# Moving the attention's product with the sigmoid from VectorE to GpSimd, with one operand of the scan in PSUM and other PSUM banks

## Chip, cores and metric

The kernel runs on one core of one Trainium2 chip (trn2). The metric is the device time of one execution, in microseconds (us). TensorE's matrix products are called PE here, its weight loads PEld, VectorE is DVE in the rows, ScalarE ACT, GpSimd POOL, and SP is the queue that issues the DMAs.

## What is computed

One decoder layer on x of shape 2048 x 1024, in float32. A projection gives the inputs of three kinds of mixer; their outputs are normalised by head group, multiplied by an output matrix, added to x and layer-normalised; then follow a feed-forward with squared relu and a second layer norm. The part that the change touches is the attention with 8 heads of 64 columns:

```python
z = jnp.einsum('bhtd,bhsd->bhts', qb, kb) * scale
mask = s_pos < t_pos
log_om = jnp.where(mask, jax.nn.log_sigmoid(-z), 0.0)
tail = lax.cumsum(log_om, axis=3, reverse=True) - log_om
log_a = jax.nn.log_sigmoid(z) + tail
a = jnp.where(mask, jnp.exp(log_a), 0.0)
outs.append(jnp.einsum('bhts,bhsd->bhtd', a, vb))
```

So the weight of position s for position t is sigmoid(z[t, s]) times the product of sigmoid(-z) over all positions between s and t.

## The kernel before

All large products are made with float32 operands split into a high and a low half, three products for each (high with high, high with low, low with high). ScalarE makes the high half by a copy, VectorE or GpSimd the low half by a subtraction. The positions are cut into four chunks of 512.

The program has two phases. Phase 1 holds the projections (`proj_t`, lines 224 to 226, and `proj_v`, lines 239 to 241), the attention, the short convolution and the pooling mixer (`bchp`), and the output product with the first layer norm (`out_stage`, product in lines 509 to 511, norm in lines 105 and 106). Phase 2 is the feed-forward (lines 656 to 679), which the change does not touch.

The attention works in score tiles, called units here: 128 positions t (index j) against up to 512 positions s of one chunk (index sg), for one head. There are 320 of them. For a head and a chunk c the tiles run from sg = c (the diagonal segment, where the four tiles are 128 to 512 wide) down to sg = 0 (each 512 wide). `unit` does this for one tile:

- PE makes z in one bank of PSUM (line 422, two products).
- ScalarE writes beta = sigmoid(-z) (line 425, one of two tiles in turn) and sig = sigmoid(z) (line 427, two tiles).
- VectorE runs a scan over beta from the right, which gives the running product in g. In the diagonal segment (line 432) the second operand is a constant tile `last`; in the other segments (line 434) the start value is one column of the g before, and the second operand is ignored, so beta is given twice.
- VectorE multiplies g by sig (line 436).

`block` then takes 128 positions s of a segment: PE transposes the four g's into one bank tp (line 453), ScalarE copies that to th (line 456), VectorE makes the low half tl (line 457), and PE adds v times th and v times tl to o (lines 458 and 459). `run` emits the blocks some five units after their tiles. `finish` takes o out (lines 472 and 473) and starts the head group's norm, whose statistics and transposes use the banks of tp too, and whose inverse root runs on VectorE in nine steps on 128 x 8 values (lines 73 to 75).

The attention uses six banks of PSUM: two for z, three for tp, one for o; the dense products have two (dn). The attention is emitted at a higher priority than the dense work of the mixers, and a scheduler, which times the program by its own model, writes each engine's order; each engine then works through its order without changing it. GpSimd has in phase 1 mostly low halves of x and of the weights (line 173: `low_engine` gives two of three to GpSimd at first and one of three to VectorE), and the sums of the pooling mixer. The transposes before the feed-forward (`transposed`, line 579) take banks of tp as well.

Of the kernel before, what the change touches and what calls it, by code (L numbers as in the profile page):

```python
# [9 lines left out]
F = mybir.dt.float32  # L10
# [3 lines left out]
ALU = mybir.AluOpType  # L14
# [3 lines left out]
P = 128  # L18
# [3 lines left out]
CH = 512  # L22
# [10 lines left out]
OFF = 8  # L33
# [8 lines left out]
def build(nc, tc, ctx, A, out):  # L42
    const = ctx.enter_context(tc.tile_pool(name="const", bufs=1))
    dram = ctx.enter_context(tc.tile_pool(name="dram", bufs=1, space=DRAM))

    nc.scalar.preload_act_table_set("sigmoid_and_others")
    ident = const.tile([P, P], F, name="ident")
    make_identity(nc, ident)
    eps_ln = const.tile([P, 1], F, name="eps_ln")
    nc.vector.memset(eps_ln, LN_EPS)  # L50

    qscr = [[dram.tile([2, HD, CH], F, name=f"qscr{c}_{h}") for h in range(HEADS)] for c in range(NC)]
    kscr = [[dram.tile([2, HD, CH], F, name=f"kscr{c}_{h}") for h in range(HEADS)] for c in range(NC)]
    vscr = [[dram.tile([4, P, 4, P], F, name=f"vscr{c}_{g}") for g in range(2)] for c in range(NC)]
    mscr = [[dram.tile([P, CH], F, name=f"mscr{c}_{j}") for j in range(ND)] for c in range(NC)]
    x1scr = [[dram.tile([P, D], F, name=f"x1scr{c}_{t}") for t in range(4)] for c in range(NC)]
    tscr = [[dram.tile([P, 4, ND, P], F, name=f"tscr{c}_{i}") for i in range(2)] for c in range(NC)]

    def split(dst_hi, dst_lo, src, scale=None):
        if scale is None:  # L60
            nc.scalar.copy(dst_hi, src)
            nc.vector.tensor_tensor(dst_lo, src, dst_hi.bitcast(F), ALU.subtract)
        else:
            nc.scalar.activation(dst_hi, src, AF.Identity, scale=scale)
            nc.vector.scalar_tensor_tensor(dst_lo, src, scale, dst_hi.bitcast(F), ALU.mult, ALU.subtract)

    def rsqrt(pool, var, eps, shape, tag):
        """1 / sqrt(var + eps): a first value from the bits of the operand, then three Newton steps."""
        v, s, t = (pool.tile(shape, F, name=f"{tag}{k}", tag=f"{tag}{k}", bufs=2) for k in "vst")
        nc.vector.tensor_scalar(v, var, eps, None, ALU.add)  # L70
        nc.vector.tensor_scalar(s.bitcast(I), v.bitcast(I), 1, 0x7FFFFFFF, ALU.logical_shift_right, ALU.bitwise_xor)
        for _ in range(3):
            nc.vector.scalar_tensor_tensor(t, s, SEED * SEED, s, ALU.mult, ALU.mult)
            nc.vector.scalar_tensor_tensor(t, t, -0.5, v, ALU.mult, ALU.mult)
            nc.vector.scalar_tensor_tensor(s, t, 1.5, s, ALU.add, ALU.mult)
        return s

    def ln_stats(p, t, inverse):
        st = p.tile([P, 2, 6], F, name="st", tag="st", bufs=2)
        for i in range(2):  # L80
            nc.vector.bn_stats(st[:, i, :], t[:, i * 512:(i + 1) * 512])
        mv = p.tile([P, 2], F, name="mv", tag="mv", bufs=2)
        nc.vector.bn_aggr(mv, st)
        return mv[:, 0:1], inverse(p, mv[:, 1:2])

    def inverse_dve(p, var):
        s = rsqrt(p, var, LN_EPS, [P, 1], "ln")
        nc.vector.tensor_scalar(s, s, SEED, None, ALU.mult)
        return s

    def inverse_act(p, var):
        y, t = (p.tile([P, 1], F, name=f"ln{k}", tag=f"ln{k}", bufs=2) for k in "yt")
        nc.scalar.activation(y, var, AF.Ln, bias=eps_ln)
        nc.scalar.activation(y, y, AF.Exp, scale=-0.5)
        nc.scalar.activation(t, y, AF.Square)
        nc.vector.scalar_tensor_tensor(t, var, LN_EPS, t, ALU.add, ALU.mult)  # L96
        nc.vector.tensor_scalar(t, t, -0.5, 1.5, ALU.mult, ALU.add)  # L97
        nc.vector.tensor_tensor(y, y, t, ALU.mult)  # L98
        return y

    def layer_norm(p, t, g, b):
        m, y0 = ln_stats(p, t, inverse_dve)
        for i in range(2):
            h = t[:, i * 512:(i + 1) * 512]
            nc.vector.scalar_tensor_tensor(h, h, m, g[i], ALU.subtract, ALU.mult)
            nc.vector.scalar_tensor_tensor(h, h, y0, b[i], ALU.mult, ALU.add)

    def bcast(p, name):
        t = p.tile([P, D], F, name=name)
        nc.sync.dma_start(t, A[name].partition_broadcast(P))  # L110
        return t

    with ExitStack() as c1:
        ff, first = phase1(nc, tc, c1, A, ident, (qscr, kscr, vscr, mscr, x1scr, tscr), split, rsqrt, layer_norm, bcast)
        phase2(nc, tc, c1, A, ff, first, x1scr, lambda p, t: ln_stats(p, t, inverse_act), bcast, out)


def phase1(nc, tc, ctx, A, ident, scr, split, rsqrt, layer_norm, bcast):
# [3 lines left out]
    pp = att.enter_context(tc.tile_pool(name="attps", bufs=1, space=PSUM, reuse_waits="tile"))  # L122
# [23 lines left out]
    for i in range(2):  # L146
        w = pd.tile([P, P], F, name=f"pw{i}")
# [26 lines left out]
        return h, l  # L174

    def load_w(g, x=None):
        """The halves of group g of w_in, with the tiles of chunk x between them as the products take them."""
        w, xt = [], []
        with early():
            for q in range(4):  # L180
                w.append(load(A["w_in"][g][q], "w", [P, 2, 256], ND))
                if x is not None:
                    xt += [load_x(x, d) for d in (2 * q, 2 * q + 1)]
        return w, xt
# [5 lines left out]
    later = []  # L190
# [11 lines left out]
        return ppd.tile([P, CH], F, name="dn", tag="dn", bufs=2)  # L202

    def operands(xs, g):
        """Yields the halves of group g of w_in with those of x for each chunk, loaded at the first use."""
        w = None
        for c, x in xs:
            if w is None:
                w, xt = load_w(g, None if x else c)
                x += xt  # L210
            elif not x:
                with early():
                    x += [load_x(c, d) for d in range(ND)]
            yield c, w, x
# [149 lines left out]
    pend, soon = [], []  # L364

    betas = []
    for i in range(2):
        t = p.tile([P, CH + 1], F, name=f"beta{i}")
# [8 lines left out]
                head(c, 2 * i + hh, mix)  # L377

    def run(end=False):
        """Emits the queued score tiles, each block of weights a few of them later."""  # L380
        while units:
            units.pop(0)()
            turn[0] += 1
            if turn[0] > 5:
                blocks.pop(0)()
        while end and blocks:
            blocks.pop(0)()
            turn[0] = 0
        while end and soon:
            soon.pop(0)[1]()  # L390
# [17 lines left out]
    def unit(c, h, sg, m, j, st, start):  # L408
# [8 lines left out]
            m.update(k=k.bitcast(R), v=v.bitcast(R), g=[])  # L417
        q = st["q"].bitcast(R)
        w = (j + 1) * P if diag else CH
        z = pp.tile([P, CH], F, name="z", tag="z", bufs=2)  # L420
        for b in range(2):
            nc.tensor.matmul(z[:, 0:w], q[:, b, j * P:(j + 1) * P], m["k"][:, 0:w], start=(b == 0), stop=(b == 1))  # L422
        beta = betas.pop(0)
# [2 lines left out]
        sig = p.tile([P, CH], F, name="sig", tag="sig", bufs=2)  # L426
# [4 lines left out]
        if diag:  # L431
            nc.vector.tensor_tensor_scan(left, rev, last[:, :CH + OFF - w - 2:-1], 0.0, ALU.mult, ALU.add)
        else:
            nc.vector.tensor_tensor_scan(left, rev, rev, st["prev"][j][:, OFF - 1:OFF], ALU.mult, ALU.bypass)  # L434
        gv = g[:, OFF:OFF + w]
        nc.vector.tensor_tensor(gv, gv, sig[:, 0:w], ALU.mult)  # L436
        st["prev"][j] = g
        m["g"].append(g)

    def block(c, h, sg, m, b, st, mix):  # L440
# [6 lines left out]
            st["o"] = pp.tile([P, CH], F, name="o", tag="o", bufs=1)  # L447
        o, v = st["o"], m["v"]
        t0 = b * P if diag else 0
        tp = pp.tile([P, CH], F, name="tp", tag="tp", bufs=3)  # L450
        cols = slice(OFF + b * P, OFF + (b + 1) * P)
        for j in range(b if diag else 0, 4):
            nc.tensor.transpose(out=tp[:, j * P:(j + 1) * P], in_=m["g"][j][:, cols], identity=ident)
# [12 lines left out]
    def finish(c, h, o, mix):  # L466
        if h % 2 == 0:
            mix["t"] = p.tile([P, CH], F, name="mixr", tag="mixr", bufs=2)
        t = mix["t"]
        own = slice((h % 2) * HD, (h % 2) * HD + HD)  # L470
        other = slice(HD - own.start, P - own.start)
        nc.scalar.copy(t[own], o[other])
        nc.vector.tensor_tensor(t[own], o[own], t[own], ALU.add)
        if h % 2:
            pend.append(rms(t, h // 2, c, lambda: pp.tile([P, CH], F, name="msp", tag="tp", bufs=3), "a"))

    wo = []

# [86 lines left out]
    def ff_pool():  # L565
        return ctx.enter_context(tc.tile_pool(name="x1", bufs=1, reuse_waits="tile"))

    spare = [(pp, 3)]

    def spare_ps():  # L570
        pool, bufs = spare[-1]
# [50 lines left out]
class FeedForward:  # L622
# [20 lines left out]
        return [[t[:, d] for d in range(ND)] for t in w]  # L643

    def hidden(self, f, w=None):
        """Squared relu of the up projection for hidden tile f, in halves."""
        nc, p = self.nc, self.p
        wh, wl = w or self.up(f)
        hh = p.tile([P, HALF], R, name="hh", tag="hh", bufs=4)
# [15 lines left out]
        return hh, hl  # L665

    def rows(self, f):
        """The rows of w_down for hidden tile f, in halves."""
        return self.split(self.pd.tile([P, D], R, name="dh", tag="dh", bufs=4),
                          self.pd.tile([P, D], R, name="dl", tag="dl", bufs=4),  # L670
                          self.raw(self.A["w_down"][f * P:(f + 1) * P, :]))
# [97 lines left out]
```

## Time and profile before

| what | value |
|---|---|
| runs, median (lowest to highest) | 2616.57 us (2616.32 to 2616.8), 3 runs |
| profiled execution: span from its first to its last instruction | 2613.2 us |
| outside the span, against the median | 3.4 us |
| mean granted clock of TensorE | 0.987 |
| first dense product, 20th unit, last unit, first product of the down projection | 4.5, 92.8, 1005.5, 1227.8 us |

The page gives for the profiled execution its span; a time of its own beside that is not listed, so the 3.4 us are the distance to the median. In the rows, a group is a line of the program, an engine, an operation, and the tiles written and read; "x" is how often. Busy time of PE is made of records that overlap, since products are pipelined.

### The profile page before, as it was taken

How to read it: one execution, taken by the hardware profiler on the slowest of the kernel's cores; microseconds unless marked ns; L12 is line 12 of the kernel's file. 1: busy time of each engine (PE TensorE's matmuls, PEld its weight loads, DVE VectorE, ACT ScalarE, POOL GpSimd, SP SyncE). 2: the span in 40 equal slices, each digit the busy share in tenths (PEclk: the TensorE clock that was granted, in tenths of full speed). 3: DMA queues.
4: the chain of work that ended last, by engine and by line, in shares of the span. 5: the costliest groups of instructions: out<-in, count | busy, mean ns of one | idle time of the engine just before them, and what ended most of it. 6: DMA issues, size and time to landing. Idle time of an engine off the chain costs nothing. (4 is left out here: it accounts for less than half of the span.)

```text
span 2613.2 us, 32747 instructions
## 1 busy us (share of the span) xinstructions
PE 2519.7 (96%) x12112; PEld 2080.0 (80%) x12112; DVE 1718.6 (66%) x2839; ACT 982.4 (38%) x1802; POOL 558.9 (21%) x293
## 2 busy tenths in 40 slices
PE   8999999889989988999999999999999999999998
PEld 7887888768767767878888888888888888888886
DVE  4899999999999998875444444443564444444437
ACT  4667666656566563212221212121332121212122
POOL 2012000330131030211221212121342121212122
PEclk9999999999999999999999999999999999999999
DMA  8658545523342342668211111110541111111111
GB/s 243 176 153 227 151 134 142 180 74 101 101 121 78 93 133 90 229 215 322 91 57 41 57 41 57 41 57 25 217 154 57 41 57 41 57 41 57 41 41 65
DMA packets 131584, 280.63 MB, mean 107 GB/s; under 512 B 14944, under 2 KB 31328, under 8 KB 130400
## 3 DMA queue, kind: packets, MB, share of 16 engines
q1 hardware_dynamic: 131424, 278.54, 33.8%
q8 instruction: 95, 1.56, 0.2%
q14 instruction: 65, 0.53, 0.1%
HBM read 211.64 MB, written 66.85 MB: 107 GB/s over the span
## 5 line engine op out<-in xcount | busy, mean ns | idle before, releaser
L704 DVE TENSOR_TENSOR y<-dn,y 128x512 f32<-128x512 f32 x448 | 303.9, 686 | 367.0 <-PE dn L679 366.6
L677 PE MATMUL dn<-dh,hh 128*128 128x512 f32 x1024 | 398.3, 389 | 0.6 <-ACT hh L662 0.6
L678 PE MATMUL dn<-dl,hh 128*128 128x512 f32 x1024 | 398.4, 389 | 0.0
L679 PE MATMUL dn<-dh,hl 128*128 128x512 f32 x1024 | 398.2, 389 | 0.0
L656 PE MATMUL up<-x,uh 128*128 128x512 f32 x1008 | 392.3, 389 | 0.0
L657 PE MATMUL up<-x,uh 128*128 128x512 f32 x1008 | 392.2, 389 | 0.0
L663 DVE SCALAR_TENSOR_TENSOR rl<-up,rl 128x512 f32<-128x512 f32 x128 | 88.5, 691 | 374.6 <-ACT hh L662 374.6
L632 POOL TENSOR_TENSOR ul<-raw,uh 128x1024 fp32r<-128x1024 f32 x63 | 152.0, 2414 | 770.1 <-PE up L659 608.5
L661 ACT ACTIVATE rl<-up 128x512 f32<-128x512 f32 x128 | 76.2, 596 | 498.0 <-PE up L659 498.0
L434 DVE TENSOR_TENSOR_SCAN g<-beta,g 128x513 f32<-128x513 f32 x192 | 257.1, 1344 | 1.4 <-ACT beta L425 1.2
L659 PE MATMUL up<-x,ul 128*128 128x512 f32 x1008 | 256.2, 389 | 0.0
L173 POOL TENSOR_TENSOR wl<-wraw,wh 128x512 fp32r<-128x512 f32 x67 | 104.6, 1567 | 622.4 <-ACT wh L171 372.1
L436 DVE TENSOR_TENSOR g<-g,sig 128x512 f32<-128x512 f32 (+2 forms) x320 | 223.1, 702 | 11.4
L677 PEld LDWEIGHTS dn<-dh,hh 128*128 128x128 f32 x1024 | 192.2, 188 | 41.2 <-ACT hh L662 1.0
L679 PEld LDWEIGHTS dn<-dh,hl 128*128 128x128 f32 x1024 | 192.1, 188 | 40.3 <-DVE hl L664 0.4
L678 PEld LDWEIGHTS dn<-dl,hh 128*128 128x128 f32 x1024 | 192.2, 188 | 39.9
L224 PE MATMUL dn<-xh,wh 128*128 128x512 f32 x512 | 211.9, 416 | 11.4 <-ACT xh L171 4.8
L659 PEld LDWEIGHTS up<-x,ul 128*128 128x128 f32 x1008 | 189.2, 188 | 39.3
L657 PEld LDWEIGHTS up<-x,uh 128*128 128x128 f32 x1008 | 189.2, 188 | 39.3
L656 PEld LDWEIGHTS up<-x,uh 128*128 128x128 f32 x1008 | 189.2, 188 | 39.2
L225 PE MATMUL dn<-xl,wh 128*128 128x512 f32 x512 | 209.9, 410 | 0.1
L425 ACT ACTIVATE beta<-z 128x512 f32<-128x512 f32 (+2 forms) x320 | 173.4, 542 | 96.7 <-PE z L422 56.0
(159 smaller groups left out, 4603.8 us busy)
## 6 DMA issues: line engine op xcount, KB each, us to landing
raw<-in_w_down SPq DMA_DIRECT2D x64, 512.0 KB, 3.3
raw<-in_w_up SPq DMA_DIRECT2D x63, 512.0 KB, 3.3
wraw<-in_w_in SPq DMA_DIRECT2D x80, 256.0 KB, 3.0
k<-kscr SPq DMA_DIRECT2D x80, 256.0 KB, 3.1
v<-vscr SPq DMA_DIRECT2D x80, 256.0 KB, 2.8
xraw<-in_xt SPq DMA_DIRECT2D x64, 256.0 KB, 3.0
q<-qscr SPq DMA_DIRECT2D x64, 256.0 KB, 4.3
x<-tscr SPq DMA_DIRECT2D x8, 2048.0 KB, 12.3
```

What stands on the lines that cost most here:

```text
L224: nc.tensor.matmul(ps, wh, xh, start=(d == 0), stop=False)
L225: nc.tensor.matmul(ps, wh, xl, start=False, stop=False)
L425: nc.scalar.activation(beta[:, CH - w:CH], z[:, 0:w], AF.Sigmoid, scale=-1.0)
L434: nc.vector.tensor_tensor_scan(left, rev, rev, st["prev"][j][:, OFF - 1:OFF], ALU.mult, ALU.bypass)
L436: nc.vector.tensor_tensor(gv, gv, sig[:, 0:w], ALU.mult)
L656: nc.tensor.matmul(ps, wh[d], xh[:, :, d, :], start=(d == 0), stop=False)
L657: nc.tensor.matmul(ps, wh[d], xl[:, :, d, :], start=False, stop=False)
L659: nc.tensor.matmul(ps, wl[d], xh[:, :, d, :], start=False, stop=(d == ND - 1))
L677: self.nc.tensor.matmul(ps, hh[:, ts], dh[:, ds], start=(i == 0), stop=False)
L678: self.nc.tensor.matmul(ps, hh[:, ts], dl[:, ds], start=False, stop=False)
L679: self.nc.tensor.matmul(ps, hl[:, ts], dh[:, ds], start=False, stop=(i == len(hid) - 1))
L704: nc.vector.tensor_tensor(y[t][:, ds], ps, y[t][:, ds], ALU.add)
```

## The change

The product of g and sig is issued on GpSimd instead of VectorE. In the segments off the diagonal the ignored second operand of the scan is the first column of z in PSUM, repeated, instead of beta; so the scan reads one tensor from SBUF and one from PSUM, and z's bank is free only when the scan is done. The bank that z gains, tp loses: three for z, two for tp, also where the norms and the transposes before the feed-forward use them.

```diff
-        z = pp.tile([P, CH], F, name="z", tag="z", bufs=2)
+        z = pp.tile([P, CH], F, name="z", tag="z", bufs=3)
...
         else:
-            nc.vector.tensor_tensor_scan(left, rev, rev, st["prev"][j][:, OFF - 1:OFF], ALU.mult, ALU.bypass)
+            idle = z[:, 0:1].to_broadcast([P, CH + 1])
+            nc.vector.tensor_tensor_scan(left, rev, idle, st["prev"][j][:, OFF - 1:OFF], ALU.mult, ALU.bypass)
         gv = g[:, OFF:OFF + w]
-        nc.vector.tensor_tensor(gv, gv, sig[:, 0:w], ALU.mult)
+        nc.gpsimd.tensor_tensor(gv, gv, sig[:, 0:w], ALU.mult)
...
-        tp = pp.tile([P, CH], F, name="tp", tag="tp", bufs=3)
+        tp = pp.tile([P, CH], F, name="tp", tag="tp", bufs=2)
...
-            pend.append(rms(t, h // 2, c, lambda: pp.tile([P, CH], F, name="msp", tag="tp", bufs=3), "a"))
+            pend.append(rms(t, h // 2, c, lambda: pp.tile([P, CH], F, name="msp", tag="tp", bufs=2), "a"))
...
-    spare = [(pp, 3)]
+    spare = [(pp, 2)]
```

The new lines shift the numbers by one: the scan stands in line 435, the product in 437, the transposes in 454, th in 457, tl in 458, the products with v in 459 and 460, the output products in 510 to 512. The scheduler writes new orders for all engines. Three places follow.

VectorE, late in the attention, before (a scan is named SCALAR_TENSOR_TENSOR in the order; tl is the low half of a transposed block, mixr and r belong to the head's end and to the output stage):

```order
L434 SCALAR_TENSOR_TENSOR g<-beta_240,g 128x513
L457 TENSOR_TENSOR tl<-tp,th 128x512 x2
L436 TENSOR_TENSOR g<-g,sig 128x512
L173 TENSOR_TENSOR xl<-xraw,xh 128x512
L434 SCALAR_TENSOR_TENSOR g<-beta_242,g 128x513
L436 TENSOR_TENSOR g<-g,sig 128x512
L434 SCALAR_TENSOR_TENSOR g<-beta_240,g 128x513
L457 TENSOR_TENSOR tl<-tp,th 128x512
L436 TENSOR_TENSOR g<-g,sig 128x512
```

The same engine in the same part of the attention, with the change:

```order
L435 SCALAR_TENSOR_TENSOR g<-beta_240,g,z 128x513
L435 SCALAR_TENSOR_TENSOR g<-beta_242,g,z 128x513
L458 TENSOR_TENSOR tl<-tp,th 128x512 x2
L435 SCALAR_TENSOR_TENSOR g<-beta_240,g,z 128x513
L458 TENSOR_TENSOR tl<-tp,th 128x512
L435 SCALAR_TENSOR_TENSOR g<-beta_242,g,z 128x513
L458 TENSOR_TENSOR tl<-tp,th 128x512
```

The products are gone from VectorE, and what is left for one unit is a scan and a low half.

PE among the last 25 units, before (dn are dense products, z scores, tp transposes, o the products with v):

```order
L422 MATMUL z<-k,q 128x512 x2
L226 MATMUL dn<-xh,wl 128x512
L224 MATMUL dn<-xh,wh 128x512
L225 MATMUL dn<-xl,wh 128x512
L226 MATMUL dn<-xh,wl 128x512
L224 MATMUL dn<-xh,wh 128x512
L453 MATMUL tp<-ident,g 128x128 x4
L458 MATMUL o<-th,v 128x512
L422 MATMUL z<-k,q 128x512 x2
L225 MATMUL dn<-xl,wh 128x512
```

PE at the same unit, with the change:

```order
L422 MATMUL z<-k,q 128x512 x2
L460 MATMUL o<-tl,v 128x512
L454 MATMUL tp<-ident,g 128x128 x3
L422 MATMUL z<-k,q 128x512 x2
L454 MATMUL tp<-ident,g 128x128 x2
L459 MATMUL o<-th,v 128x512
L460 MATMUL o<-tl,v 128x512
```

The dense products that stood between the units are earlier in the order now: more of them stand between the first 241 units, and none between the last 79.

GpSimd in the first part of the attention, with the change (xl and wl are low halves of x and of the weights):

```order
L173 TENSOR_TENSOR wl<-wraw,wh 128x512
L437 TENSOR_TENSOR g<-g,sig 128x512
L173 TENSOR_TENSOR wl<-wraw,wh 128x512
L437 TENSOR_TENSOR g<-g,sig 128x512 x4
L437 TENSOR_TENSOR g<-g,sig 128x128
L437 TENSOR_TENSOR g<-g,sig 128x256
L437 TENSOR_TENSOR g<-g,sig 128x384
```

Before, this engine's order had one low half after another there; now the products stand between them.

## Rows read from the trace of the kernel before

**Rows 1.** The page's part 1: busy us, share of the span, instructions.

```profile
PE 2519.7 (96%) x12112; PEld 2080.0 (80%) x12112; DVE 1718.6 (66%) x2839; ACT 982.4 (38%) x1802; POOL 558.9 (21%) x293
```

**Rows 2.** The page's part 2: busy tenths in 40 slices of the span.

```profile
PE   8999999889989988999999999999999999999998
...
DVE  4899999999999998875444444443564444444437
```

**Rows 3.** Four stretches: length, busy us by engine (instructions), clock, DMA share, GB/s.

```profile
4.50:92.80 88.30, 84.60 (x473) 72.39 (x473) 51.40 (x79) 44.95 (x95) 15.86 (x12) 1.00 0.81 235
92.80:1005.50 912.70, 846.75 (x4597) 698.02 (x4596) 886.51 (x1482) 579.09 (x1187) 175.91 (x111) 0.97 0.45 129
1005.50:1227.80 222.30, 216.24 (x997) 174.63 (x997) 165.60 (x412) 46.96 (x82) 32.82 (x21) 0.99 0.65 228
1227.80:2613.20 1385.40, 1372.11 (x6050) 1134.91 (x6049) 613.90 (x860) 309.15 (x438) 332.82 (x139) 1.00 0.19 65
```

**Rows 4.** PE's slots: group of transposes, four in the timeline, 100 us of feed-forward.

```profile
L453 PE MATMUL tp<-ident,g 128*128 128x128 f32 x1043 | 179.3, 278 | 20.4 <-DVE tl L457 9.1 <-DVE g L436 6.8 <-DVE oa L291 4.3
...
428.51 0.60 PE L453 MATMUL tp<-ident,g 128*128 128x128 f32 x4
...
1300.00:1400.00 100.00, 100.00 (x443) 82.81 (x442) 41.75 (x56) 20.63 (x28) 23.22 (x10) 1.00 0.15 49
```

**Rows 5.** Waits of PE, 92.8 to 1005.5 us: us in total, times, longest.

```profile
PE o L459 <- DVE tl L457: 23.4, 29, 2.6
PE tp L453 <- DVE tl L457: 9.1, 7, 3.1
...
PE dn L224 <- DVE cs L354: 2.2, 2, 1.6
```

**Rows 6.** VectorE, same stretch: line 434's group, then lines 436, 432, 173, 75, 73.

```profile
L434 DVE TENSOR_TENSOR_SCAN g<-beta,g 128x513 f32<-128x513 f32 x190 | 254.6, 1344 | 1.4 <-ACT beta L425 1.2
...
92.80:1005.50 912.70, 211.10 (x300) 0.97 0.45 129
...
92.80:1005.50 912.70, 96.10 (x110) 0.97 0.45 129
...
92.80:1005.50 912.70, 43.22 (x46) 0.97 0.45 129
...
92.80:1005.50 912.70, 21.61 (x90) 0.97 0.45 129
...
92.80:1005.50 912.70, 17.77 (x91) 0.97 0.45 129
```

**Rows 7.** Single lines on VectorE, with the shortest/median/longest ns of one.

```profile
L434 DVE TENSOR_TENSOR_SCAN g<-beta,g x192: 1256/1278/2386, 98.5 to 1010.2; 128x513 f32<-128x513 f32 x192
...
L436 DVE TENSOR_TENSOR g<-g,sig x320: 255/680/1784, 59.5 to 1012.7; 128x512 f32<-128x512 f32 x96, 128x128 f32<-128x128 f32 x32, 128x384 f32<-128x384 f32 x32
...
L457 DVE TENSOR_TENSOR tl<-tp,th x305: 257/676/692, 95.3 to 1002.7; 128x512 fp32r<-128x512 f32 x92, 128x128 fp32r<-128x128 f32 x31, 128x384 fp32r<-128x384 f32 x30
...
L75 DVE SCALAR_TENSOR_TENSOR rmsas<-rmsat,rmsas x45: 133/156/1190, 107.5 to 961.5; 128x8 f32<-128x8 f32 x45
```

**Rows 8.** Timeline of GpSimd and VectorE: start, us, operation, times.

```profile
466.24 7.01 POOL L173 TENSOR_TENSOR xl<-xraw,xh 128x512 fp32r<-128x512 f32 x4 [63.17 <-ACT xh L171]
...
465.02 0.42 DVE L457 TENSOR_TENSOR tl<-tp,th 128x256 fp32r<-128x256 f32 x1
465.36 3.45 DVE L434 TENSOR_TENSOR_SCAN g<-beta,g 128x513 f32<-128x513 f32 x2
468.74 3.37 DVE L436 TENSOR_TENSOR g<-g,sig 128x512 f32<-128x512 f32 x2
```

**Rows 9.** GpSimd's line 173 in the stretch: one row by length, then its groups.

```profile
L173 POOL TENSOR_TENSOR wl<-wraw,wh x45: 1270/1604/2605, 123.5 to 972.3; 128x512 fp32r<-128x512 f32 x45
...
L173 POOL TENSOR_TENSOR wl<-wraw,wh 128x512 fp32r<-128x512 f32 x45 | 73.6, 1639 | 406.2 <-ACT wh L171 270.8 <-DMA kscr<-qk 34.6 <-ACT th L456 32.4
L173 POOL TENSOR_TENSOR xl<-xraw,xh 128x512 fp32r<-128x512 f32 x42 | 67.5, 1623 | 259.4 <-ACT xh L171 239.4 <-PE tp L453 12.0 <-DMA xraw<-in_w_o 4.6
```

## The prediction, made before any run of the changed kernel

> **What bounds the kernel now.** I read the page first: PE is busy 96% of the span, VectorE 66%, GpSimd 21% [rows 1]. A share over the whole span hides the stages, so next the slices: in the first 15 of 40, which is the attention, VectorE stands at 9 tenths nearly throughout while PE dips to 7 or 8; afterwards PE stands at 9 and VectorE falls to 4 [rows 2]. The stretches make it exact [rows 3]: from 92.8 to 1005.5 us VectorE is busy 886.5 of 912.7 us, 97%. PE shows 846.8 us there, but its records overlap, so I count slots instead. In the feed-forward 443 products of 512 columns start in 100 us, so a slot is 0.226 us; narrower products go in proportion; four 128x128 transposes take 0.60 us and one record is 0.28, so a slot is (0.60 - 0.28) / 3 = 0.11 us [rows 4]. The order of the kernel before has in that stretch 2716 products (as 512-wide ones) and 1285 transposes and small statistics products: 614 + 141 = 755 us of PE's work in 912.7 us. So VectorE sets the pace of the attention, and PE that of what follows: in the 222.3 us up to the feed-forward PE has 206 us of slots, a ratio of 1.08.
>
> PE's own waits in the attention point the same way: the list has nine rows, from 23.4 to 2.2 us and 62 us together, and all but one are for VectorE [rows 5].
>
> **What the change takes off VectorE.** The product with the sigmoid leaves it: 300 products, 211.1 us in the stretch [rows 6]. Alone, one takes 0.68 us (the median), but the longest took 1.78 [rows 7]. Why is seen where GpSimd works [rows 8]: while GpSimd does four tensor operations in 7.01 us, two scans take 3.45 us in place of 2.56 and two products 3.37 in place of 1.36. An operation of VectorE with two SBUF inputs and one of GpSimd exclude each other. The low half tl, with one input in PSUM, shows none of it: median 0.676 us, longest 0.692 [rows 7]. Even an 8-element step of the norms goes from 0.156 to 1.19 us [rows 7].
>
> I price these waits as the time above the undisturbed one [rows 6, 7]: scans 254.6 - 190 x 1.28 = 11 us; products 211 - 183 = 28 (217 of 0.68 us, and 83 narrower ones at an estimated 0.43); first-segment scans 96.1 - 110 x 0.80 = 8 (1.28 in proportion to 321 columns on average); halves of x and weights 43.2 - 46 x 0.68 = 12; steps of the norms 59.8 - 272 x 0.156 = 17 (three lines, 21.6 to 17.8 us). That is 76 us for 918 starts, with GpSimd busy 175.9 / 912.7 = 19.3% of the time [rows 3], so 76 / (918 x 0.193) = 0.43 us for each expected meeting.
>
> After the change the starts with two SBUF inputs are 110 first-segment scans, 46 halves and 272 steps, 428 in all; the 190 other scans drop out, since their ignored operand is read from PSUM. GpSimd gets the products: at 1.27 us for 512 columns, its fastest row [rows 9], and in proportion for the narrower ones, 300 make about 340 us. With its present 176 less its own waits, 111 x 0.3, it is busy 482 of some 920 us, 52%. Waits: 428 x 0.52 x 0.43 = 96 us. VectorE is left with 886.5 - 211 - (76 - 28) + 96, and an estimated 22 us for the layer norm of chunk 0, which the new order moves into the attention: 745 us. GpSimd at 52% is no bound, and 0.6 us more for a product matters only if somebody waits for it.
>
> A scan that reads PSUM is not in the trace. The nearest rows are tl (PSUM and SBUF, 0.676) and the product (SBUF twice, 0.680) [rows 7]: no difference, so I take 0. As bounds I use the 0.06 us by which the two kinds of scan differ, 190 x 0.06 = 11 us either way.
>
> **What becomes the bound.** The order on PE tells. Units are score tiles, 320 of them. In the new order the last 79 have no dense product between them. In four parts, at the slots above: up to unit 20, 66 us (78 before); units 20 to 241 with the dense products, 2615 products and 982 transposes, 591 + 108 = 699 us; the bare units 242 to 320, 285 products and 308 transposes, 98 us; the end, 175 us (206 before). The sum, 1040 us, is the same in both, so what counts is how much PE stands still.
>
> - Lead: 88.3 us now [rows 3], less (78 - 66) x 1.14, its present ratio: 75 us.
> - Filled part: 699 x 1.08, the ratio of the stretch where PE is the bound, is 757 us. VectorE has 745 - 79 x 1.96 = 590 us there, so it is behind only in places. I add 25 us, two fifths of PE's present 62 us of waits [rows 5].
> - Bare part: PE needs 98 us for 79 units, VectorE a scan and a low half for each, 1.28 + 0.68 = 1.96. I take 2.0 us: 158 us. It can't be below 79 x 1.82 = 144 (VectorE's operations overlap by some 0.08 us where nothing holds them, as 465.02 + 0.42 against 465.36 [rows 8]); I set the other end at 2.5 us, 198, since the loop through ScalarE, VectorE, GpSimd and the transposes has no other work to hide in, and PE, with gaps, may be granted less clock, as it is in the attention now (0.97 against 1.00 [rows 3]).
> - End: 175 x 1.08 = 189 us. The feed-forward is untouched: 1385.4 us [rows 3].
>
> Sum with the 4.5 us before the first product: 4.5 + 75 + 782 + 158 + 189 + 1385.4 = 2593.9, against the span of 2613.2: 19 us less. Outside the span lie 3.4 us to the median of the runs, 2616.6, so 2598 us.
>
> **Banks and queues.** Three banks for z cover that the scan now holds its bank: at 2 us for a unit, a bank is free again about 3 us after its product (ScalarE 0.61 twice, then the scan), and three give 6. Two banks for tp give 4 us for a hold of 0.5 + 0.6 + 0.68 and a wait for one scan, 3.1 us. I cost both at nothing; were that cover gone, PE's waits for a bank of tp are at most 9.1 us now [rows 5], and a doubling is 9 us. The sig tiles are now freed by GpSimd, 1.3 us later; ScalarE, at 579 of 912.7 us [rows 3], has the room.
>
> **The rivals.**
> *VectorE no longer counts.* If its waits fall where PE has work anyway, the 25 us go and the bare part comes at 144: 2559 us. For it speaks that VectorE has 745 us of some 915. Chance 0.15.
> *Waits take it back.* If each of the 428 starts that meets GpSimd waits for a whole product, 428 x 0.52 x 1.28 = 285 us, VectorE has 937 us, as much as PE's two parts (940), and they don't overlap perfectly: some 20 us more, 2618 us, no change. Against it stands the measured 0.43. The Trainium skill (SBUF — State Buffer, Who interferes with whom) says that whoever starts first keeps the shared ports for its whole instruction; by that rule this rival is the ceiling, and the rows agree on the waiting but not on its full length. Chance 0.12.
> *GpSimd's queue holds the products up: slower.* GpSimd works in order, and 87 of its halves of x and weights stand in the stretch [rows 9], now between products, as the order shows. It now waits for ScalarE's copies before them for 270.8 and 239.4 us in all [rows 9], which costs nothing as nothing is behind. Each such wait now holds the products behind it, then the transposes, then PE, which is in order too. At 0.22 us for each half the 19 us are gone; at 0.6 us, half a product, 87 x 0.6 = 52 us: 2650 us. Against it: the new order puts a half only where ScalarE's copy is due. The Trainium skill (GPSIMD Engine Reference, Engine selection) advises against two-input elementwise work on GpSimd, as about twice as slow; the rows agree (1.27 against 0.68 us), and by that advice alone this rival would be the outcome. Chance 0.20.
> *The scans aren't freed.* If PSUM in the second place doesn't keep a scan from the meetings, 190 x 0.52 x 0.43 = 42 us come on top for VectorE, at least half of them on the path: 2619 to 2640 us. tl's row is against it. Chance 0.08.
>
> **How the numbers follow.** The forecast itself has 0.45. A measurement of this kernel can tell 0.2% (5 us) from no change. Faster: 0.45 + 0.15 = 0.60. Within 0.2%: 0.12. Slower: 0.20 + 0.08 = 0.28. The range reaches from the gaining rival (2559, less 3 for the scans) to most of the slower one, 2642; its own bounds from the bare part, 2584 to 2638, lie inside. About 2 in 10 are left out, most of it above.
>
> **What would show it.** Right: VectorE near 80% in the attention, offset scans at 1.28 us whatever GpSimd does, L437 near 1.3 us on GpSimd, PE with few gaps up to about 930 us and then some 160 us of gaps at 2 us a unit. Wrong: PE waiting for GpSimd's g by tens of us; scans still up to 2.3 us; bare units well over 2.5 us; VectorE still at 95%.

## The result and the profile after

The changed kernel takes 2645.62 us (median; 2644.76 to 2651.29), the kernel before 2616.45 beside it: a ratio of 1.0118, 95% interval [1.0103, 1.0132]. It is slower by 1.2%. The prediction was 2598 us with a range of 2556 to 2642 and 0.60 on faster: the sign is wrong and the time lies just above the range.

The page's part 1 and two lines of part 2 of the kernel after, to be held against [rows 1, 2]:

```profile
PE 2535.1 (96%) x12112; PEld 2082.8 (79%) x12112; DVE 1588.8 (60%) x2519; ACT 990.3 (37%) x1802; POOL 918.8 (35%) x613
...
PE   8999999998998888999999999999999999999998
...
DVE  4677768888789889786334343434564443444437
```

VectorE lost 130 us of busy time (1718.6 to 1588.8) and is no longer at 9 tenths throughout; GpSimd gained 360. The share of PE is the same 96%. So the load moved as the edit says, and the time still went up. The stretches of the kernel after, cut where the prediction cuts (columns as in [rows 3]; up to unit 20, filled part up to the 242nd unit, before which the last dense product stands, bare part, end, feed-forward):

```profile
5.00:83.00 78.00, 74.38 (x390) 62.65 (x391) 37.74 (x49) 37.26 (x77) 29.79 (x25) 0.98 0.83 237
83.00:895.80 812.80, 769.88 (x4176) 642.88 (x4175) 644.48 (x1057) 474.36 (x959) 424.66 (x339) 0.98 0.47 135
895.80:1059.00 163.20, 132.29 (x638) 92.15 (x637) 148.49 (x202) 123.72 (x252) 99.98 (x83) 0.96 0.33 92
1059.00:1257.60 198.60, 186.63 (x866) 150.40 (x866) 142.80 (x343) 43.01 (x75) 29.90 (x19) 0.97 0.66 233
1257.60:2642.90 1385.30, 1371.81 (x6049) 1134.66 (x6047) 613.66 (x860) 309.44 (x438) 333.00 (x139) 1.00 0.19 65
```

Against the terms of the sum: lead 78.0 (75), filled part 812.8 (782), bare part 163.2 (158), end 198.6 (189), feed-forward 1385.3 (1385.4). With 0.5 us more ahead of the first product that is 49 us too much, 31 of them in the filled part; the bare part, at 2.07 us a unit, came nearly as priced (2.0). VectorE is at 79% in the filled part, where some 80% were foreseen, and at 91% in the bare one. What was not foreseen are its idle times. Its own waits in the kernel after, 83 to 1059 us (engine, what waits, for what; us in total, times, longest), then PE's:

```profile
DVE tl L458 <- ACT th L457: 50.6, 43, 4.7
DVE g L435 <- PE tp L454: 27.4, 16, 5.1
DVE g L432 <- PE tp L454: 15.6, 12, 3.4
DVE g L435 <- ACT sig L427: 15.0, 22, 2.3
```

```profile
PE o L460 <- DVE tl L458: 24.6, 24, 3.4
PE z L422 <- DVE g L435: 20.3, 38, 2.1
```

In the kernel before, VectorE hardly waited at all in the attention (97% busy, [rows 3]). Now it stands in front of tl until ScalarE has made th (50.6 us), and in front of scans until transposes have freed a g buffer (27.4 and 15.6). Both wait for the transposes (th is their copy), the place where the change took a bank away.

### The profile page after: what moved, and what is told of

Same layout as the page of the kernel before. It is cut to its first block, busy times and chain, and to the rows that moved or that the text cites. A ratio compares the mean times of both kernels' runs of the same rounds, so it can differ in the third digit from the quotient of the medians.

```text
span 2642.9 us, 32912 instructions
## 1 busy us (share of the span) xinstructions
PE 2535.1 (96%) x12112; PEld 2082.8 (79%) x12112; DVE 1588.8 (60%) x2519; ACT 990.3 (37%) x1802; POOL 918.8 (35%) x613
## 5 line engine op out<-in xcount | busy, mean ns | idle before, releaser
L437 POOL TENSOR_TENSOR g<-g,sig 128x512 f32<-128x512 f32 (+2 forms) x320 | 389.0, 1226 | 386.1 <-DVE g L435 193.1
L435 DVE TENSOR_TENSOR_SCAN g<-beta,g,z 128x513 f32<-128x513 f32 x192 | 241.5, 1273 | 42.9 <-PE tp L454 27.4
L633 POOL TENSOR_TENSOR dl<-raw,dh 128x1024 fp32r<-128x1024 f32 x64 | 153.6, 2402 | 252.9 <-ACT dh L632 252.9
L422 PE MATMUL z<-k,q 128*128 128x512 f32 (+3 forms) x640 | 196.2, 393 | 28.4 <-DVE g L435 20.3
## 6 DMA issues: line engine op xcount, KB each, us to landing
x<-tscr SPq DMA_DIRECT2D x8, 2048.0 KB, 11.9
```

The source lines that it names most:

```text
L435: nc.vector.tensor_tensor_scan(left, rev, idle, st["prev"][j][:, OFF - 1:OFF], ALU.mult, ALU.bypass)
L437: nc.gpsimd.tensor_tensor(gv, gv, sig[:, 0:w], ALU.mult)
L633: self.nc.gpsimd.tensor_tensor(lo, raw, hi.bitcast(F), ALU.subtract)
```

## The experiments

All of them compute the full output. The edits are written against the changed kernel ("change"); the short names are z for the score tiles' banks and tp for the transposes'.

**The three edits taken apart (e1 to e4).** With each, the scheduler also makes another order, above all of the dense products: in the change the last one ahead of the last score tile stands at unit 241, in the kernel before at 317. In every run with the banks of the change that is left to its own order the unit is 239 to 241 (the change, e3, e4, e12), in the others 293 to 319 (before, e1, e2, e8, e10, e11): the bank edits bring the early order. The first theory was that this order is the loss.

e1, the product on GpSimd alone (last dense product at unit 319; msp, a tile of the norms' statistics, goes with tp's banks):

```diff
-            idle = z[:, 0:1].to_broadcast([P, CH + 1])
-            nc.vector.tensor_tensor_scan(left, rev, idle, st["prev"][j][:, OFF - 1:OFF], ALU.mult, ALU.bypass)
+            nc.vector.tensor_tensor_scan(left, rev, rev, st["prev"][j][:, OFF - 1:OFF], ALU.mult, ALU.bypass)
...
-        z = pp.tile([P, CH], F, name="z", tag="z", bufs=3)
+        z = pp.tile([P, CH], F, name="z", tag="z", bufs=2)
...
-        tp = pp.tile([P, CH], F, name="tp", tag="tp", bufs=2)
+        tp = pp.tile([P, CH], F, name="tp", tag="tp", bufs=3)
...
-    spare = [(pp, 2)]
+    spare = [(pp, 3)]
```

> The product on GpSimd alone: both scan operands from SBUF, 2 banks for z, 3 for tp. The order on PE is then that of the kernel before (dense products up to unit 319). Theory 'order' (the loss is the early spending of the dense products, which leaves 79 score tiles bare): VectorE loses 211 us and gains some 60 us of waits, PE's 755 us of slots in the attention take 1.08 to 1.15 times that, so 2520 to 2570 us, faster than before. Theory 'GpSimd' (the product's 1.3 us, its queue and the waits for the shared port cost what VectorE is spared): 2610 us or more.

Measured 2622.12 us, ratio 1.0023 [1.0014, 1.0032]: the time that theory "GpSimd" gave, a miss for theory "order". e2 undoes the banks alone: of e1's diff, the six lines on z, tp and spare, and msp.

> The product on GpSimd and the scan's ignored operand from PSUM, with the banks of before (z 2, tp 3). The last dense product stands at unit 303, not 241. Theory 'order': units 20 to 320 hold 789 us of slots, at 1.1 times 868 us, lead 80, end 190: about 2540 us. Theory 'GpSimd': 2610 us or more. A third, 'banks of z' (the scan holds its bank, so two are too few): PE's waits for z at 100 us or more and a time above 2600.

Measured 2600.74 us, 0.9939 [0.9924, 0.9954]: faster than before, by 15.7 us, though not the 2540 of theory "order"; PE's waits for z are 17.4 us in its row below, not 100, so z's banks are out. The two edits without the banks are a gain, and the banks, with the order that they bring, cost 2645.62 - 2600.74 = 44.9 us. e3 (the change with the scan of e1) and e4 (the banks alone) look at them from the other side.

e3 has the three lines on the scan; e4 has them too, and

```diff
-        nc.gpsimd.tensor_tensor(gv, gv, sig[:, 0:w], ALU.mult)
+        nc.vector.tensor_tensor(gv, gv, sig[:, 0:w], ALU.mult)
```

> As the change, but both operands of the scan from SBUF again. The order is nearly that of the change (last dense product at unit 239). Theory 'order': about the time of the change, plus up to half of 190 x 0.52 x 0.43 = 42 us of waits where VectorE sets the pace: 2645 to 2670. If the scan's hold of the z bank is what costs (theory 'banks of z'), it is faster than the change: below 2630.

> The banks alone: z 3, tp 2, product and scan as before. The last dense product stands at unit 239. Theory 'order': the attention of before with 80 bare units at VectorE's 2.7 us each (216 us) after a filled part of 740 us of slots at 1.1 to 1.15: some 2690 us, 2660 to 2720, clearly slower than before. Theory 'GpSimd': the banks are nothing, 2616 within 10 us.

e3: 2735.34 us, 1.0451 [1.0433, 1.0468], 65 us above what was expected: the scan's operand is worth far more than I priced, 89.7 us with these banks. e4: 2715.34 us, 1.0377 [1.0361, 1.0392], within its range: the banks alone cost the old kernel 99 us.

**Is it the order of the dense products, or the banks (e5, e6)?** The order was now tied: a table of the products for z and dn in the order wanted, and for each pair of neighbours an edge that only orders issue on PE. The core of it (`log` holds PE's products as the program makes them):

```python
for a, b in zip(order, order[1:]):
    tc.add_manual_dep(log[b], log[a].name, after, reason="order")
```

e5 is the change with e2's order, e6 is e2 with the change's.

> The change as it is (z 3 banks, tp 2), with the order of z and dense products on PE tied, by edges that only order issue, to that of e2, whose last dense product stands at unit 303. Theory 'order' (the two tp banks cost 45 us only by making the dense products come early): the time of e2, 2595 to 2610. Theory 'tp' (two banks hold up the transposes themselves): still 2635 to 2650.

> The reverse: e2 (z 2 banks, tp 3) with the order of z and dense products tied to that of the change, last dense product at unit 241. Theory 'order': the time of the change, 2635 to 2655. Theory 'tp': the time of e2, 2595 to 2610.

e5: 2643.44 us, 1.0102 [1.0087, 1.0117]; e6: 2651.93 us, 1.0133 [1.0116, 1.0150]. Each theory is met in one run and fails in the other. The two bank edits at the even order cost as much (42.7 us) as with the early one (44.9), and so does the early order without them (51.2): the two costs don't add up. So theory "order" falls as it stood, and what the two have in common had to be found. The tie holds z and dn alone; the transposes and o are placed anew in each run, and e2 with its own order tied wasn't run.

**What two tp banks do (e9, e13).** A block's path is: transposes, th on ScalarE, tl on VectorE, two products o. I counted, from the order of PE's records in the traces and at the prediction's slots, how much of PE's work stands between the last transpose of a block and its first product o. In e2 the median of the 320 blocks is 5.7 us and the tenth percentile 2.6; in the change 3.7 and 0.9, in e5 3.8 and 0.9, in e9 and e13 3.7 and 1.0. In e6 it is 4.6 and 1.8, but 2.0 in the median behind unit 241, where e2 has 4.8. In the traces of both e2 and the change the path from the start of th to the end of tl takes 2.0 us in the median and about 4 in the slowest tenth. So with the short distance PE, which is in order, gets to o too soon. With two banks the transposes of a third block need a bank that tl has left, so they hardly ever stand between: transposes of two or more other blocks begin there in 195 of the 320 blocks in e2, in 22 in e9. e9 takes one tp bank from e2 and nothing else; e13 gives all three back but ties the whole order on PE, transposes and o included, to that of e9.

Against e2 at its tied order, e9 has (msp again with it)

```diff
-        tp = pp.tile([P, CH], F, name="tp", tag="tp", bufs=3)
+        tp = pp.tile([P, CH], F, name="tp", tag="tp", bufs=2)
...
-    spare = [(pp, 3)]
+    spare = [(pp, 2)]
```

> e2 with its order of z and dense products tied and tp cut to 2 banks; z stays at 2, so one bank is unused. It is e5 without the third z bank. Theory 'tp' (two banks put each block's o product sooner behind its transposes: by PE's slots the tenth percentile of that distance is 1.0 us here and 2.5 in e2, while ScalarE's copy and VectorE's subtraction need 1.2 alone): 2635 to 2665, with PE's waits of o for tl at 20 us or more. If the third z bank is what costs in e5: 2595 to 2610.

> e2 with its three tp banks, but the whole order on PE (transposes and o products too) tied to that of e9. Theory 'distance' (what two banks do is to put o sooner behind its transposes): the time of e9, 2620 to 2640. Theory 'hold' (a transpose waits for the bank): the time of e2, 2595 to 2610.

e9: 2630.29 us, 1.0045 [1.0030, 1.0060], 5 us below its range, and PE's waits of o for tl are 11.9 us, not 20; e13: 2627.02 us, 1.0042 [1.0027, 1.0057], as theory "distance" has it. A bank less costs 29.6 us at the same order of dense products; and with the bank back, but the order that two banks make, 26.3 of them remain. It is the order that the banks force, and hardly the wait for a bank. That it costs by this distance is what the rows below support, and not shown apart: e13 ties the whole of PE's order, and the orders that the scheduler then gave VectorE and ScalarE are e9's too, but for 8 of 2519 and 2 of 1802 places. e2's stretch from unit 20 to 320 and its end, then its waits, VectorE's and PE's:

```profile
95.00:1023.40 928.40, 878.23 (x4745) 724.26 (x4743) 794.05 (x1249) 579.38 (x1197) 517.08 (x418) 0.97 0.46 132
1023.40:1214.10 190.70, 182.53 (x850) 147.11 (x850) 137.47 (x339) 40.62 (x71) 27.57 (x18) 0.99 0.69 241
```

```profile
DVE g L435 <- ACT sig L427: 46.8, 59, 3.0
DVE g L432 <- ACT beta L425: 19.9, 22, 1.6
DVE tl L458 <- ACT th L457: 14.7, 23, 2.1
...
PE z L422 <- DVE g L435: 17.4, 20, 3.3
PE o L460 <- DVE tl L458: 5.5, 7, 1.7
```

The same of e13 (its line numbers are 116 higher, by the table):

```profile
94.00:1044.60 950.60, 880.98 (x4738) 725.30 (x4736) 780.12 (x1250) 590.13 (x1197) 518.46 (x419) 0.98 0.44 129
1044.60:1242.30 197.70, 186.41 (x860) 150.33 (x860) 141.10 (x340) 41.74 (x73) 28.75 (x18) 0.97 0.66 232
```

```profile
DVE tl L574 <- ACT th L573: 51.5, 42, 5.4
DVE g L551 <- PE tp L570: 18.5, 16, 4.5
...
PE o L576 <- DVE tl L574: 13.4, 20, 2.0
```

tl's wait for th goes from 14.7 to 51.5 us and the scans wait for transposes: the rows of the change, in a kernel with three banks. VectorE's wait grows by more than PE's own for tl (5.5 to 13.4). The end, too, is 7 us longer (190.7 to 197.7), as it is in the change (198.6): its transposes of x1 use tp.

**What the two other edits are worth (e14, e15; also e10).** At e2's tied order, one of them taken back each: e14 has the scan's three lines of e1's diff, e15 the product's two of e4's. e10 is e15 with its own order (last dense product at unit 293).

> e2 at its tied order, with the scan's ignored operand from SBUF again. If the operand is worth what the traces of e1 and e2 show (57 us of meetings with GpSimd saved, 47 us of new waits for sig, since the scan on z waits for sig's end): within 10 us of e2. If the meetings alone count: 2625 to 2660.

> e2 at its tied order, with the product on VectorE again. If the product on GpSimd pays where the order is even: 2620 to 2660. If what it takes off VectorE comes back as meetings and as 1.3 us more in each tile's chain: within 10 us of e2.

> The scan's PSUM operand alone, product on VectorE, banks of before. Theory 'GpSimd pays' (VectorE keeps some 870 us in the attention and its 97%): 2605 to 2625. Theory 'GpSimd gives nothing' (what it takes off comes back as waits): the time of e2, 2595 to 2605.

e14: 2644.16 us, 1.0112 [1.0097, 1.0127], as if the meetings with GpSimd alone counted: the operand is worth 43 us where GpSimd has the product and the order is e2's. With each run's own order it is 21 us (e1 against e2), and 9 us where VectorE has the product (e10 against the kernel before). e15: 2606.33 us, 0.9968 [0.9954, 0.9982], within 10 us of e2: the move of the product is worth 6 us, though VectorE has 888 us of 935 busy in e15 and 794 of 928 in e2. e10: 2607.46 us, 0.9966 [0.9953, 0.9980], 7 us above e2, at the lower edge of what "GpSimd pays" gave. It pays little, even where the order is even.

The offset scan in e1, in the kernel after and in e14, as shortest/median/longest or as a mean:

```profile
L434 DVE TENSOR_TENSOR_SCAN g<-beta,g x192: 1228/1290/2396, 98.5 to 1021.2; 128x513 f32<-128x513 f32 x192
```

```profile
L435 DVE TENSOR_TENSOR_SCAN g<-beta,g,z x192: 1251/1273/1286, 104.5 to 1062.6; 128x513 f32<-128x513 f32 x192
```

```profile
L491 DVE TENSOR_TENSOR_SCAN g<-beta,g 128x513 f32<-128x513 f32 x189 | 293.0, 1559 | 24.5 <-ACT beta L482 21.2 <-PE tp L510 1.5 <-POOL g L493 1.2
```

From PSUM none of 192 takes more than 1.286 us; from SBUF the mean is 1.559 (e14), against 1.276 in e2, so 189 x 0.283 = 53 us for the scans. The 43 us at the end are what remains when e14 is spared e2's waits of scans for sig (46.8 us above) and has other waits in their place.

**The waits in the norms (e7, e8, e11, e12).** In e2 the stretches in which the norms are computed are still slow. There VectorE works through chains of small steps with both operands in SBUF. e7 keeps the variance and the step's own product in the PSUM tile where the variance is computed, so that one operand comes from PSUM (the three factors are grouped differently for that); the order is tied to e2's. `rsqrt` takes the two tiles as v and t for it.

```diff
...
-            nc.vector.scalar_tensor_tensor(t, s, SEED * SEED, s, ALU.mult, ALU.mult)
-            nc.vector.scalar_tensor_tensor(t, t, -0.5, v, ALU.mult, ALU.mult)
+            nc.vector.scalar_tensor_tensor(t, v, SEED * SEED, s, ALU.mult, ALU.mult)
+            nc.vector.scalar_tensor_tensor(t, t, -0.5, s, ALU.mult, ALU.mult)
...
-                y = rsqrt(pool, var[:, 0:8], RMS_EPS, [P, 8], f"rms{who[0]}")
+                y = rsqrt(pool, var[:, 0:8], RMS_EPS, [P, 8], f"rms{who[0]}", var[:, 8:16], var[:, 16:24])
```

> e2 with its order tied, and in the RMS norms' Newton steps one operand of each kept in the PSUM tile that holds the variance (the same product in another grouping), so that no step reads SBUF alone. In e2 the steps L71 and L73 to L75 took 63 us above their undisturbed time between 93 and 1025 us. Theory 'waits in the norms' (they fall where VectorE sets the pace, in the stretches with norms): 40 to 60 us less than e2, 2540 to 2560. Theory 'hidden' (PE has work there): within 10 us of e2.

> As e7, with the order left to the scheduler (last dense product at unit 315). Theory 'waits in the norms': as e7 or some us less, 2530 to 2560, since there is hardly a bare part. Theory 'hidden': 2590 to 2605.

e7: 2568.32 us, 0.9823 [0.9807, 0.9839], 32 us less than e2; e8, with its own order: 2562.12 us, 0.9790 [0.9776, 0.9805], the fastest of all. Theory "waits in the norms" names the place, but 63 us of waits gave 32, not 40 to 60. One line of these steps in e2, and the line in its place in e7:

```profile
L73 DVE SCALAR_TENSOR_TENSOR rmsat<-rmsas x48: 136/167/1300, 107.5 to 1147.1; 128x8 f32<-128x8 f32 x48
```

```profile
L131 DVE SCALAR_TENSOR_TENSOR msp<-msp,rmsas x48: 150/174/175, 105.6 to 1114.3; 128x8 f32<-128x8 f32 x48
```

Units 200 to 220, in e2 and in e7:

```profile
638.00:715.50 77.50, 67.63 (x332) 54.09 (x331) 71.40 (x110) 48.44 (x97) 53.09 (x41) 0.91 0.43 130
```

```profile
627.80:696.20 68.40, 62.56 (x330) 50.58 (x329) 58.83 (x108) 46.63 (x95) 50.82 (x40) 1.00 0.50 146
```

The longest step falls from 1.300 to 0.175 us. VectorE goes from 71.4 of 77.5 us (92%) to 58.8 of 68.4 (86%), and PE, with fewer gaps, has the clock granted in full: 1.00 in place of 0.91, a mean between its two levels of 1.2 and 2.4 GHz. The same edit in the kernel before, and in the change:

> The kernel before with the norms' steps as in e7. There L71 and L73 to L75 took 21 us above their undisturbed time. Theory 'waits in the norms': at most those 21 us, 2595 to 2612. If the steps gain by their new form itself, and not by the missed meetings: as much as in e7, 32 us, 2585 or less.

> The change with the norms' steps as in e7 (last dense product at unit 239, tp 2). In the change L71 and L73 to L75 took 55 us above their undisturbed time. Theory 'waits in the norms': 25 to 55 us off, 2590 to 2620. Theory 'hidden' (the two tp banks hold PE up in any case): 2635 to 2650.

e11: 2620.83 us, 1.0018 [1.0008, 1.0027]: nothing gained, 4 us lost, where GpSimd is busy 20% of the time, so it isn't the steps' new form that pays. But theory "waits in the norms" (at most 21 us less) missed too, though VectorE has less to do: 868.4 of 916.8 us in e11, 886.5 of 912.7 before. e12: 2633.48 us, 1.0061 [1.0039, 1.0082]: 12 us off the change, too little for "waits in the norms" (25 to 55) and 1.5 us below the range of "hidden". That the two tp banks hide the rest is not shown.

## Why the prediction was wrong, point by point

- **The filled part: the step that failed.** "Filled part: 699 x 1.08, the ratio of the stretch where PE is the bound", and "25 us" for waits, gave 782 us; 812.8 came, 31 of the 49 us. About 13 us are the count: between the 20th and the 242nd unit the trace shows 1094 transposes and small products, not 982 (each small statistics product is two records), and 112 x 0.11 x 1.08 = 13. (Two slips in the sums change little: 699 x 1.08 is 755, not 757, and in the second rival 745 - 96 + 285 is 934, not 937.) The rest is PE standing still. By the slots, as an estimate, PE has 714 us of work there and stands 99 us, 0.45 us a unit; in e2, at an even order, it has 803 of 928 us and stands 0.42 us a unit. So the dense products brought forward filled no gaps: PE takes 1.14 times its slots, and VectorE with 79% doesn't set the pace either. The two wait for each other.
- **The order as a whole.** I took it as given and priced its parts one by one; I did not ask what the same work costs at an even order. e6 shows it: 51 us more than e2 with only z and dn re-ordered. Its bare units (second row) cost what I said, 157.5 for 158 us; PE stands some 0.75 us for each, by the slots, and still 0.53 for each of the filled part (first row), so that part pays nothing back. That the order costs by the short distance behind unit 241 is the likeliest reading; it was not shown.

```profile
85.00:919.50 834.50, 779.95 (x4207) 647.70 (x4206) 641.73 (x1064) 469.69 (x964) 419.58 (x339) 0.98 0.46 132
919.50:1077.00 157.50, 133.05 (x625) 92.02 (x623) 144.67 (x197) 120.42 (x249) 99.98 (x83) 0.93 0.33 94
```

- **Banks: the other step that failed.** "Two banks for tp give 4 us for a hold of ... 3.1 us. I cost both at nothing; were that cover gone, ... a doubling is 9 us." The two bank edits cost 44.9 us with the order that they bring and 42.7 at the even one (e5 against e2), tp's alone 29.6 (e9 against e2). I asked whether a bank is free in time, on the average. What counts is that fewer banks change the order: o stands closer behind the transposes (median 3.7 us in place of 5.7), and a path of 2.0 us in the median is about 4 in its slowest tenth. e13 shows, with the bank given back, that the order is enough. At the change's own order of z and dn, giving the banks back gains nothing (e6 is 6 us above the change), so the 49 us can't be split between this step and the one before. Why a third z bank, added to two of tp, takes 13 us more (e5 against e9) stays open: from 94 to 1040 us ScalarE waits less for z in e5 (18.9 us against 79.2), PE for z's banks no less (23.5 against 23.3), and it wasn't tried apart.
- **VectorE as what sets the pace of the attention.** That was read from its 97% [rows 3]. The runs don't bear it out for the attention as a whole: e2 takes 94 us of work off VectorE against e15 and is 6 us faster, e11 takes 18 off the kernel before and is no faster.
- **The waits for the port: right in size, wrong in place.** I had 96 us in 428 starts; by the same count (time above the undisturbed one, in the same three groups) the kernel after has 92 in 468. But I let VectorE's spare time in the filled part take them, since it has 590 of 782 us to do there on the average. They stand bunched in the stretches with norms, where VectorE has the least room (92% in the row of e2 above): without 63 of them e2 is 32 us faster (e7).
- **The scan from PSUM: right, with a wait missed.** It costs nothing more by itself (1.273 us) and doesn't meet GpSimd; the rival "the scans aren't freed" is out, and the operand is the best part of the change (43 us by e14, 21 by e1). Missed was that ScalarE reads the same bank for sig: in the program the scan now waits for the end of sig instead of beta's. In e1 67 of 192 offset scans start before sig has ended, in e2 and in the change none; e2 waits 46.8 us for it. The Trainium skill (PSUM — Partial Sum Buffer, PSUM bank collisions raise a hardware error) says that two engines may not access one bank in the same partitions at the same time, reads included, and that their accesses are to be ordered by semaphores; the trace agrees, the shortest gap from sig's end to the scan is 0.03 us. Two scans with their sigmoids, in e1 the scan 0.03 us after beta's end (596.23) and ahead of sig's (596.72), in e2 0.04 us after sig's (326.00):

```profile
595.65 0.58 ACT L425 ACTIVATE beta<-z 128x512 f32<-128x512 f32 x1
596.13 0.59 ACT L427 ACTIVATE sig<-z 128x512 f32<-128x512 f32 x1
596.26 1.29 DVE L434 TENSOR_TENSOR_SCAN g<-beta,g 128x513 f32<-128x513 f32 x1
```

```profile
324.92 0.60 ACT L425 ACTIVATE beta<-z 128x512 f32<-128x512 f32 x1
325.41 0.59 ACT L427 ACTIVATE sig<-z 128x512 f32<-128x512 f32 x1
326.04 1.28 DVE L435 TENSOR_TENSOR_SCAN g<-beta,g,z 128x513 f32<-128x513 f32 x1
```

- **The product on GpSimd.** Its length was right (1.334 us against 1.27), its worth was not: I booked 211 us off VectorE as the source of the gain; by e15 it is 6 us. The Trainium skill (Perfetto Trace Analysis, Optimizing Scalar/DVE Operations) warns that moving work between these two engines may not help, since they share a port; e15 and e2 agree in the outcome, and no run shows how much of it is the port.
- **GpSimd's queue, the rival with this time (2650).** That its time is near is no proof of it. Its mechanism is not what decided: the halves' waits for ScalarE are 36.5 + 19.7 = 56 us in the kernel after, but 9.1 + 10.1 = 19 in e9, hardly more than e2's 16, and e9 is still 30 us slower than e2. What those 37 us add in the change was not tried.

```profile
L173 POOL TENSOR_TENSOR wl<-wraw,wh 128x512 fp32r<-128x512 f32 x53 | 74.7, 1416 | 46.9 <-ACT wh L171 36.5 <-PE dn L511 4.1 <-PE dn L225 3.7
L173 POOL TENSOR_TENSOR xl<-xraw,xh 128x512 fp32r<-128x512 f32 x42 | 56.7, 1364 | 25.5 <-ACT xh L171 19.7 <-PE dn L241 3.6 <-PE tp L454 1.6
```

- **The end** (198.6 for 189) is the order that the tp banks force again: 190.7 in e2 and e6, 198.4 in e9. The feed-forward was right to 0.1 us. That e2, the change without its bank edit, comes at 2600.7 beside my 2598 is no merit of the sum: it has another order, with other terms.

## What to carry to other kernels

A buffer taken away is not priced by asking whether it is free in time on the average: look at the order that comes of it, at how much other work the new order still puts between a producer's start and its consumer on the in-order engine, and hold its lower tail against the upper tail of the path. Work moved ahead in an order need not fill gaps there: price the order as a whole against an even one, and waits by the stretch in which they fall. A high busy share alone does not show that an engine sets the pace. And take a bundle of edits apart before judging it: here two edits gain 16 us and the third costs 45; with the norms' steps moved to PSUM and the banks left alone the same idea takes 2562 us, 2.1% less than before.

## What had not been expected of the hardware

Not only operations with two SBUF inputs meet GpSimd. L71 has one SBUF input and two constants, and in the kernel after its longest takes 1.303 us at a median of 0.171:

```profile
L71 DVE TENSOR_SCALAR rmsas<-rmsav x16: 139/171/1303, 110.6 to 1189.1; 128x8 int32<-128x8 int32 x16
```

Eleven of the 32 such steps on 128 x 8 values took over 0.3 us, and each of them ended some 0.03 us after an operation of GpSimd that ran beside it. In e7, where the input comes from PSUM, none took over 0.168. The Trainium skill (SBUF — State Buffer, Who interferes with whom) names tensor_scalar, copy and cast among the operations that can take the shared port; the row agrees, and my count of 428 starts had left them out.
